# More of the mixer's weight splitting on GpSimd, and another order for the products behind it

## The chip, the cores and the metric

The kernel runs on one core of a Trainium2 chip. Time is microseconds of device time for one execution, the median of three runs. The core's engines are TensorE (PE, with PEld for its weight loads), VectorE (DVE), ScalarE (ACT), GpSimd (POOL) and SyncE (SP), which issues the transfers. Each works through its own queue in order and waits on semaphores of the others.

## What is computed

Two layers over a sequence of 256 rows of 1024 numbers, all in float32. A layer is a SwiGLU feed-forward block (FFN, 2816 wide) at half weight, a token mixer, and a second FFN; after each the sum with the scaled input goes through a layer norm. The mixer projects the row once and feeds three groups of heads:

```python
z = x @ w_in
y_sc  = sc_b * depthwise_conv(sc_c * sc_h, sc_conv_w)        # 3 taps, 256 channels
y_att = banded_window_attention(q, k, v, attn_sink)          # 8 query heads, 2 key heads of 64
u = depthwise_conv(cc_a * sigmoid(cc_gate), cc_conv_w) + cc_conv_b   # 31 taps, 256 channels
y_cc = silu(layer_norm(u, cc_ln_g, cc_ln_b))
out = concatenate([y_sc, y_att, y_cc]) @ w_out
```

## The kernel before

The 256 rows are two tiles of 128 (t = 0, 1). All weights come from HBM as 156 blocks of 128 x 2048 float32 (1 MB), in the order in which they are used. A product of float32 precision is made of three products in a shorter format: each operand is split into a high part (a cast, on ACT, L96) and a low part (operand minus high part, L97), and `mm3` (L153 to L155) adds high x high, low x high and high x low. `emit_block` splits the next block into two of five pairs of buffers; a pair is free for block i when the products with block i-5 have read it. `release` asks for the next split when a block's last product has been issued. In the mixer and at the ends of the FFNs the split goes in four quarters of 128 x 512.

A layer has 33 blocks for the first FFN, 12 for the mixer and 33 for the second FFN. Of the mixer's, 0 and 1 hold the convolution's gate and input, 2 and 3 the queries, 4 keys and values, 5 to 7 the short convolution's three inputs, 8 to 11 the rows of `w_out` (`W_OUT` says which group of heads uses which). In layer 0 they have the numbers 33 to 44 in the order below, so that mixer block 4 is block 37, and blocks 45 to 48 are the first four of the second FFN. Which low parts GpSimd makes instead of DVE is set by `ON_POOL`, counted from the mixer's start:

```python
ON_POOL = range(7, 16)
POOL_BLOCKS = [l * (2 * PER_FFN + PER_MIX) + PER_FFN + i for l in range(DEPTH) for i in ON_POOL]
```

In the mixer TensorE projects and transposes while ACT and DVE do the softmax of four units u (two tiles by two key heads): `S_` scores, `N_` the normalised exponentials, `T_` their transposes, `V_` the product with the values. The 31-tap convolution is 62 DVE instructions (L531, L533), which `fill` puts in portions between the rest. When it is done, `cc_norm` transposes its result and norms it (the reciprocal root on GpSimd, L611), and `cc_out` transposes back, applies swish and splits: that is y[3], the convolution's part of the last product. `w_out(t, h, i)` is six products of head group i for tile t and half h of the 1024 columns; `w_out2(t, i)` does both halves.

Behind the mixer and each FFN but the last stands `boundary`: `part` gives the last products of tile 0, `gather` adds them to the scaled input and takes statistics, `stats` makes the variance on DVE and its reciprocal root on GpSimd (`rstd`, L228), and `apply` scales in two steps on DVE: L233 without the root, L234 with it. Meanwhile TensorE does the products of tile 1. Then `turn(0, h)` transposes the finished tile 0 (L205, reading `x`), and ACT and DVE split it for the next stage. Tile 1 follows in the same way while the next stage's projections (`proj_n`, L181, L182, L185) run on tile 0: `turn(1, 0)` comes behind three of its blocks, `turn(1, 1)` behind the fourth. The order in each queue is what the framework's scheduler makes of the order in which the code is written.

Of the kernel before, what the change touches and what calls it, by code (L numbers as in the profile page):

```python
# [38 lines left out]
PER_MIX = 12  # L39
NBLOCKS = DEPTH * (2 * PER_FFN + PER_MIX)  # L40
W_OUT = (1, 2, 0, 3)
ON_POOL = range(7, 16)
POOL_BLOCKS = [l * (2 * PER_FFN + PER_MIX) + PER_FFN + i for l in range(DEPTH) for i in ON_POOL]


@with_exitstack
def encoder(ctx: ExitStack, tc: tile.TileContext, head_in, xt_in, x_in, w_in, gb_in, small_in, rope_in, out):
# [25 lines left out]
    def big():  # L73
        return hpool.tile([P, 512], F32, tag="big", bufs=6, name="big")

    def bank():
        return acc.tile([P, 512], F32, tag="acc", name="bank")
# [10 lines left out]
    def tmp_bank():  # L88
        return phase["pool"].tile([P, 512], F32, tag="mm", name="tmp")
# [5 lines left out]
    def split(hi, lo, src, eng=None):  # L95
        nc.scalar.copy(hi, src)  # L96
        (eng or nc.vector).tensor_tensor(lo, src, hi.bitcast(F32), ALU.subtract)  # L97
# [42 lines left out]
    def release(delay=2):  # L140
        tasks.append((state["tick"] + delay, emit_block))
# [5 lines left out]
    def tick(parts=1):  # L147
        state["tick"] += 1
        while tasks and tasks[0][0] <= state["tick"]:
            tasks.pop(0)[1](parts)  # L150

    def mm3(ps, ah, al, bh, bl, first, last):
        nc.tensor.matmul(ps, ah, bh, start=first, stop=False)  # L153
        nc.tensor.matmul(ps, ah, bl, start=False, stop=False)  # L154
        nc.tensor.matmul(ps, al, bh, start=False, stop=last)  # L155
# [47 lines left out]
    def transpose(ps, srcs):  # L203
        for i, a in enumerate(srcs):
            nc.tensor.transpose(ps[:, i * P:(i + 1) * P], a, ident)  # L205
# [252 lines left out]
    def mixer(l, norm):  # L458
# [64 lines left out]
        def emit_conv():  # L523
            cacc = chan(big())
            pacc = [tmp_bank() for _ in range(2)]

            def tap(k, c):
                part = pacc[c][:, 0:S]
                dst = cacc[:, c, :] if k == WCC - 1 else part
                if k == 0:  # L530
                    nc.vector.tensor_scalar(dst, upad[:, c, 0:S], wc2[:, c, 0:1], b_cc[:, c:c + 1], op0=ALU.mult, op1=ALU.add)  # L531
                else:
                    nc.vector.scalar_tensor_tensor(dst, upad[:, c, k:k + S], wc2[:, c, k:k + 1], part, op0=ALU.mult, op1=ALU.add)  # L533

            for k in range(WCC):
                for c in range(2):
                    conv.append(lambda k=k, c=c: tap(k, c))
            return cacc
# [51 lines left out]
        def attend(t, i, pT):  # L590
            tk = slice(t * P, (t + 1) * P)
            po = tmp_bank()
            for j in range(2):
                hp = slice(j * HD, (j + 1) * HD)
                for kt in range(NT):
                    nc.tensor.matmul(po[hp, 0:2 * P], vn[kt][:, hp], pT[j][:, kt * 2 * P:(kt + 1) * 2 * P], start=kt == 0, stop=kt == NT - 1)  # L596
            split(y[i][0][:, :, tk], y[i][1][:, :, tk], chan(po[:, 0:2 * P]))

        def cc_norm():
            pus = [tmp_bank() for _ in range(NT)]  # L600
            stat, uns = [], []
            for t, pu in enumerate(pus):
                transpose(pu, [cacc[:, c, t * P:(t + 1) * P] for c in range(2)])
                sts = st.tile([P, 6], F32, tag="sts1", name="sts1")
                mv = st.tile([P, 2], F32, tag="mv", name="mv")
                ve = st.tile([P, 1], F32, tag="ve", name="ve")
                rstd = st.tile([P, 1], F32, tag="rstd", name="rstd")
                nc.vector.bn_stats(sts, pu[:, 0:2 * P])
                nc.vector.bn_aggr(mv, sts)
                nc.vector.tensor_scalar_add(ve, mv[:, 1:2], EPS)  # L610
                nc.gpsimd.tensor_tensor(rstd, ve, mhalf, ALU.pow)  # L611
                stat.append((mv, rstd))
            for pu, (mv, rstd) in zip(pus, stat):
                un = big()
                nc.vector.tensor_scalar(un[:, 0:2 * P], pu[:, 0:2 * P], mv[:, 0:1], rstd, op0=ALU.subtract, op1=ALU.mult)
                uns.append(un)
            return uns

        def cc_out(uns):
            vv, tv = big(), big()  # L620
            for t, un in enumerate(uns):
                pv = tmp_bank()
                transpose(pv, [un[:, 0:P], un[:, P:2 * P]])
                for c in range(2):
                    nc.vector.tensor_scalar(chan(vv)[:, c, t * P:(t + 1) * P], pv[:, c * P:(c + 1) * P], gb2[:, c:c + 1], gb2[:, 2 + c:3 + c],
                                            op0=ALU.mult, op1=ALU.add)
            nc.scalar.activation(tv, vv, AF.Tanh)
            nc.vector.scalar_tensor_tensor(tv, tv, 1.0, vv, op0=ALU.add, op1=ALU.mult)
            split(y[3][0], y[3][1], chan(tv))
# [49 lines left out]
        def T_(u):  # L679
            pTs[u] = p_turned(prs.pop(u)[0])  # L680

        def V_(u):
            attend(u // 2, u % 2, pTs.pop(u))
# [48 lines left out]
        def w_out(t, h, i, ks=(0, 1)):  # L732
            tk = slice(t * P, (t + 1) * P)
            cs = slice(h * 512, (h + 1) * 512)
            for c in ks:
                mm3(accs[t][h], y[i][0][:, c, tk], y[i][1][:, c, tk], wo[W_OUT[i]][0][:, c, cs], wo[W_OUT[i]][1][:, c, cs],
                    (t, h) not in begun, i == 3 and c == 1)
                begun.add((t, h))

        def w_out2(t, i):  # L740
            for h in range(2):
                w_out(t, h, i)
            if t == 1:
                release(1)
            tick()
# [1 line left out]
        w_out2(0, 0)  # L747
        fill(62)
        T_(3)
        w_out2(0, 2)  # L750
        uns = cc_norm()
        V_(3)
        accs.append([bank() for _ in range(2)])
        new_norm = Norm()
        w_out2(1, 2)
        cc_out(uns)
        w_out2(1, 0)
        w_out2(0, 1)

        def part(t, h, piece, cs=(0, 1)):  # L760
            if t == 0:
                if piece == 1:
                    w_out(0, h, 3)
            else:
                w_out(1, h, (1, 3)[piece], cs)
                if h == 1 and 1 in cs:
                    release()

        boundary(accs, new_norm, part)
        return new_norm  # L770

# [3 lines left out]
    for l in range(DEPTH):  # L775
        norm = ffn(l == 0, norm, False)
        norm = mixer(l, norm)
        norm = ffn(False, norm, l == DEPTH - 1)
# [85 lines left out]
```

## Time and profile before

| | |
|---|---|
| median of 3 runs | 935.26 us (935.13 to 937.06) |
| the profiled execution | 937.28 us, span 935.5 us |
| busy: PE, DVE, ACT, POOL | 99%, 69%, 49%, 12% of the span |
| granted clock of TensorE | 0.995 on the mean |
| the two mixers | about 188 to 290 and 650 to 751 us |

The profiled execution's own time is 1.78 us more than its span, which counts from the first to the last instruction of the core. Times below are microseconds from the span's start. A PE that is shown busy is not at its peak: a row of a product is drawn 0.39 us long where the next starts 0.23 us after it.

### The profile page before, as it was taken

To read this page: it belongs to the slowest core of one execution; us is meant where nothing else is said; L and a number is where in the kernel's file an instruction comes from. 1 tells how busy PE (TensorE), PEld (TensorE's weight loads), DVE (VectorE), ACT (ScalarE), POOL (GpSimd) and SP (SyncE) were. 2 spreads that over 40 slices of the span, in tenths; PEclk is the share of its full clock that TensorE was granted. 3 is DMA by queue.
4 is the path that set the end of the run, shared out by engine and by line. 5 is a ranking of instruction groups with operands and counts; after the bars stand their busy time and mean duration, and the time that the engine had idled before them with its cause. 6 is when DMAs were issued, how large, how long until landed. Compare 5 with 4: busy or idle time off the path is not lost.

```text
span 935.5 us, 12113 instructions
## 1 busy us (share of the span) xinstructions
PE 921.8 (99%) x4900; PEld 778.7 (83%) x4900; DVE 645.4 (69%) x811; ACT 458.1 (49%) x593; POOL 116.9 (12%) x108
## 2 busy tenths in 40 slices
PE   9999999999999999999999999999999999999996
PEld 6888888888777888888888888888887788888885
DVE  6966556789967756665777665667799766666545
ACT  6644554345744554445345445454456455444530
POOL 0010000009282000000000000000274800000000
PEclk9999999999999999999999999999999999999998
DMA  9976465546234655454456545544551366555301
GB/s 345 376 249 257 175 222 183 180 140 224 88 102 181 257 211 195 178 187 177 179 187 230 213 180 198 202 171 150 216 190 57 139 247 224 189 180 188 128 1 45
DMA packets 25976, 174.01 MB, mean 186 GB/s; under 512 B 2880, under 2 KB 3136, under 8 KB 5696
## 3 DMA queue, kind: packets, MB, share of 16 engines
q1 hardware_dynamic: 25920, 173.24, 51.5%
q8 instruction: 38, 0.62, 0.3%
q14 instruction: 18, 0.15, 0.0%
HBM read 172.18 MB, written 1.05 MB: 185 GB/s over the span
## 4 chain that ended last, share of the span: by engine, by line
PE 88%; DVE 7%; ACT 1%; POOL 1%; issue 1%; DMA 1%; SPq 0%; DVEq 0%; ACTq 0%
PE wide L170 28%; PE wide L174 15%; PE bank L153 9%; PE bank L154 9%; PE bank L155 9%; PE bank L181 4%; PE bank L185 4%; PE bank L182 4%; DVE tmp L533 3%; PE bank L195 1%; PE tmp L205 1%; POOL lo L97 1%; PE tmp L596 1%; PE bank L205 1%; DVE x L234 1%
## 5 line engine op out<-in xcount | busy, mean ns | idle before, releaser
L97 DVE TENSOR_TENSOR lo<-raw,hi 128x2048 fp32r<-128x2048 f32 (+2 forms) x175 | 317.1, 1825 | 211.1 <-ACT hi L96 210.8
L96 ACT CAST hi<-raw 128x2048 fp32r<-128x2048 f32 (+2 forms) x247 | 306.4, 1270 | 241.2 <-PE wide L170 154.2
L170 PE MATMUL wide<-xT,hi 128*128 128x512 f32 x1152 | 274.1, 390 | 0.0
L170 PEld LDWEIGHTS wide<-xT,hi 128*128 128x128 f32 x1152 | 213.9, 188 | 43.0
L174 PEld LDWEIGHTS wide<-xT,lo 128*128 128x128 f32 x1152 | 147.7, 191 | 5.6
L174 PE MATMUL wide<-xT,lo 128*128 128x256 f32 x1152 | 149.4, 283 | 0.0
L153 PE MATMUL bank<-hi,hh 128*128 128x512 f32 x352 | 137.7, 391 | 0.0
L154 PE MATMUL bank<-lo,hh 128*128 128x512 f32 x352 | 137.4, 390 | 0.0
L155 PE MATMUL bank<-hi,hl 128*128 128x512 f32 x352 | 137.0, 389 | 0.0
L97 POOL TENSOR_TENSOR lo<-raw,hi 128x512 fp32r<-128x512 f32 x72 | 95.9, 1366 | 67.2 <-ACT hi L96 66.8
L228 POOL TENSOR_TENSOR rstd<-ve,mhalf 128x1 f32<-128x1 f32 x12 | 11.5, 961 | 672.0 <-DVE ve L227 672.0
L155 PEld LDWEIGHTS bank<-hi,hl 128*128 128x128 f32 x352 | 66.1, 188 | 14.0
L153 PEld LDWEIGHTS bank<-hi,hh 128*128 128x128 f32 x352 | 66.2, 188 | 12.7
L154 PEld LDWEIGHTS bank<-lo,hh 128*128 128x128 f32 x352 | 66.2, 188 | 12.3
L96 ACT CAST hh<-big 128x512 fp32r<-128x512 f32 x36 | 22.3, 620 | 110.2 <-DVE big L358 110.2
L181 PE MATMUL bank<-hi,xT 128*128 128x512 f32 x160 | 64.7, 404 | 0.0
L182 PE MATMUL bank<-lo,xT 128*128 128x512 f32 x160 | 62.6, 391 | 0.0
L366 DVE TENSOR_TENSOR big<-wide,big 128x512 f32<-128x512 f32 x72 | 49.2, 684 | 6.9 <-ACT big L365 6.9
L533 DVE SCALAR_TENSOR_TENSOR tmp<-upad,wc,tmp 128x256 f32<-128x256 f32 x116 | 49.7, 477 | 0.2
L365 ACT COPY big<-wide 128x512 f32<-128x512 f32 x72 | 42.3, 587 | 11.9 <-PE wide L174 11.6
L185 PE MATMUL bank<-hi,xT 128*128 128x512 f32 x160 | 43.2, 392 | 0.0
L97 DVE TENSOR_TENSOR hl<-big,hh 128x512 fp32r<-128x512 f32 x36 | 24.9, 693 | 24.0 <-ACT hh L96 24.0
(130 smaller groups left out, 890.5 us busy)
## 6 DMA issues: line engine op xcount, KB each, us to landing
raw<-in_w SPq DMA_DIRECT2D x152, 1024.0 KB, 4.8
gb<-in_gb SPq DMA_DIRECT2D x6, 1024.0 KB, 4.9
raw<-in_w SPq DMA_DIRECT2D x4, 512.0 KB, 7.5
head<-in_head SPq DMA_DIRECT2D x4, 384.0 KB, 4.6
raw<-in_w SPq DMA_DIRECT2D x4, 256.0 KB, 7.7
x<-in_x SPq DMA_DIRECT2D x2, 512.0 KB, 5.7
out<-x SPq DMA_DIRECT2D x4, 256.0 KB, 2.1
xraw<-in_xt SPq DMA_DIRECT2D x2, 256.0 KB, 8.0
```

The source lines that it names most:

```text
L96: nc.scalar.copy(hi, src)
L97: (eng or nc.vector).tensor_tensor(lo, src, hi.bitcast(F32), ALU.subtract)
L153: nc.tensor.matmul(ps, ah, bh, start=first, stop=False)
L154: nc.tensor.matmul(ps, ah, bl, start=False, stop=False)
L155: nc.tensor.matmul(ps, al, bh, start=False, stop=last)
L170: nc.tensor.matmul(ps[:, c], w[0][:, k, cs], xT[:, :, k], start=k == 0, stop=False)
L174: nc.tensor.matmul(ps[:, c, 0], w[1][:, k, cs], xT_h[:, k], start=False, stop=k == KC - 1)
L181: nc.tensor.matmul(ps, xT_h[:, kk, t, :], w[0][:, k, :], start=kk == 0, stop=False)
L182: nc.tensor.matmul(ps, xT_h[:, kk, t, :], w[1][:, k, :], start=False, stop=False)
L185: nc.tensor.matmul(ps, xT_l[:, kk, t, :], w[0][:, k, :], start=False, stop=kk == KC - 1)
L366: nc.vector.tensor_tensor(av, ps[:, :, 0], av, ALU.add)
L533: nc.vector.scalar_tensor_tensor(dst, upad[:, c, k:k + S], wc2[:, c, k:k + 1], part, op0=ALU.mult, op1=ALU.add)
```

## The change

`ON_POOL` begins at 4: GpSimd also makes the low parts of the mixer's blocks 4 to 6 (the fifth to the seventh), 12 instructions of 128 x 512 a layer. Between the attention and the boundary the calls change places: `cc_norm` and `V_(3)` come ahead of `w_out2(0, 2)`, `cc_out` comes right behind that, and the two products that stood around it follow. The products of tile 1 with the first attention group, `w_out(1, h, 0)`, leave this place and go into `part` of the boundary, ahead of the others of tile 1. No computation is added or taken away.

```diff
@@ -39,7 +39,7 @@
 PER_MIX = 12
 NBLOCKS = DEPTH * (2 * PER_FFN + PER_MIX)
 W_OUT = (1, 2, 0, 3)
-ON_POOL = range(7, 16)
+ON_POOL = range(4, 16)
 POOL_BLOCKS = [l * (2 * PER_FFN + PER_MIX) + PER_FFN + i for l in range(DEPTH) for i in ON_POOL]
 
 
@@ -747,21 +747,24 @@
         w_out2(0, 0)
         fill(62)
         T_(3)
-        w_out2(0, 2)
         uns = cc_norm()
         V_(3)
+        w_out2(0, 2)
+        cc_out(uns)
         accs.append([bank() for _ in range(2)])
         new_norm = Norm()
+        w_out2(0, 1)
         w_out2(1, 2)
-        cc_out(uns)
-        w_out2(1, 0)
-        w_out2(0, 1)
 
         def part(t, h, piece, cs=(0, 1)):
             if t == 0:
                 if piece == 1:
                     w_out(0, h, 3)
             else:
+                if piece == 0:
+                    w_out(1, h, 0)
+                    if h == 1:
+                        release()
                 w_out(1, h, (1, 3)[piece], cs)
                 if h == 1 and 1 in cs:
                     release()
```


GpSimd's queue at the end of layer 0's first FFN, before; `rstd_782` is the root for tile 0 and `rstd_783` that for tile 1, and the number behind `lo` is the block's:

```order
L228 TENSOR_TENSOR rstd_782<-ve_1512,mhalf_92 128x1
L228 TENSOR_TENSOR rstd_783<-ve_1555,mhalf_92 128x1
L97 TENSOR_TENSOR lo40_1785<-raw40_1580,hi40_1784 128x512 x4
L97 TENSOR_TENSOR lo41_1836<-raw41_1592,hi41_1835 128x512 x4
```


The same place with the change:

```order
L228 TENSOR_TENSOR rstd_782<-ve_1512,mhalf_92 128x1
L97 TENSOR_TENSOR lo37_1595<-raw37_1378,hi37_1594 128x512 x4
L228 TENSOR_TENSOR rstd_783<-ve_1555,mhalf_92 128x1
L97 TENSOR_TENSOR lo38_1730<-raw38_1420,hi38_1729 128x512 x4
L97 TENSOR_TENSOR lo39_1765<-raw39_1466,hi39_1764 128x512 x4
```


The four quarters of block 37 now stand between the two roots. GpSimd's queue at the end of layer 0's mixer, before; `rstd_2426` belongs to tile 0, `rstd_2427` to tile 1:

```order
L97 TENSOR_TENSOR lo46_2441<-raw46_1845,hi46_2440 128x512 x3
L464 TENSOR_SCALAR gb2_5428<-small_94 128x4
L97 TENSOR_TENSOR lo46_2441<-raw46_1845,hi46_2440 128x512
L97 TENSOR_TENSOR lo47_2481<-raw47_1927,hi47_2480 128x512 x4
L228 TENSOR_TENSOR rstd_2426<-ve_2520,mhalf_92 128x1
L97 TENSOR_TENSOR lo48_2579<-raw48_2041,hi48_2578 128x512 x4
L228 TENSOR_TENSOR rstd_2427<-ve_2563,mhalf_92 128x1
```


The same place with the change, where the two roots are `rstd_2454` and `rstd_2455`:

```order
L464 TENSOR_SCALAR gb2_5440<-small_94 128x4
L97 TENSOR_TENSOR lo46_2481<-raw46_1857,hi46_2480 128x512 x4
L228 TENSOR_TENSOR rstd_2454<-ve_2508,mhalf_92 128x1
L97 TENSOR_TENSOR lo47_2579<-raw47_1939,hi47_2578 128x512 x4
L97 TENSOR_TENSOR lo48_2591<-raw48_2053,hi48_2590 128x512 x4
L228 TENSOR_TENSOR rstd_2455<-ve_2563,mhalf_92 128x1
```


Block 47 has gone behind the first root, so that two blocks instead of one stand ahead of the second. TensorE's queue there with the change, from the last product that reads block 42 to the first turn of tile 0 (`x0`):

```order
L155 MATMUL bank_2447<-hi42_1929,yhl_1618 128x512
L153 MATMUL bank_2447<-hi43_2043,yhh_1619 128x512
L154 MATMUL bank_2447<-lo43_2044,yhh_1619 128x512
L155 MATMUL bank_2447<-hi43_2043,yhl_1620 128x512
L153 MATMUL bank_2447<-hi43_2043,yhh_1619 128x512
L154 MATMUL bank_2447<-lo43_2044,yhh_1619 128x512
L155 MATMUL bank_2447<-hi43_2043,yhl_1620 128x512
L153 MATMUL bank_2447<-hi44_2185,yhh_1623 128x512
L154 MATMUL bank_2447<-lo44_2186,yhh_1623 128x512
L155 MATMUL bank_2447<-hi44_2185,yhl_1624 128x512
L205 MATMUL tmp_2551<-ident_85,x0_649 128x128 x4
```


Before, block 42's last product of this kind stood at the end of `w_out2(1, 0)`, ahead of all of tile 0's last products; now nine products are left between it and the turn.

## Rows read from the trace of the kernel before

**Rows 1.** The page, part 1: busy time of each engine, share of the span, instructions
```profile
PE 921.8 (99%) x4900; PEld 778.7 (83%) x4900; DVE 645.4 (69%) x811; ACT 458.1 (49%) x593; POOL 116.9 (12%) x108
```

**Rows 2.** Waits of TensorE in layer 0's mixer, 186:300: total us, times, longest us
```profile
PE tmp L205 <- DVE x L234: 1.1, 2, 0.7
PE bank L548 <- ACT pr L564: 0.6, 2, 0.4
```

**Rows 3.** The same view for layer 1's mixer, 648:760
```profile
PE tmp L205 <- DVE x L234: 0.6, 2, 0.4
```

**Rows 4.** Timeline of TensorE, end of layer 0's mixer: start, us, line, tiles [idle <- by]
```profile
278.70 0.39 PE L154 MATMUL bank<-lo,yhh 128*128 128x512 f32 x1
278.93 0.39 PE L155 MATMUL bank<-hi,yhl 128*128 128x512 f32 x1
...
280.05 0.66 PE L205 MATMUL tmp<-ident,x 128*128 128x128 f32 x4 [0.74 <-DVE x L234]
...
281.01 0.40 PE L155 MATMUL bank<-hi,yhl 128*128 128x512 f32 x1
...
281.74 0.66 PE L205 MATMUL tmp<-ident,x 128*128 128x128 f32 x4 [0.33 <-DVE x L234]
...
290.74 0.60 PE L205 MATMUL tmp<-ident,x 128*128 128x128 f32 x4
```

**Rows 5.** Timeline of TensorE, attention of layer 0, then of layer 1
```profile
235.44 1.75 PE L205 MATMUL bank<-ident,pr 128*128 128x128 f32 x8
...
237.59 0.70 PE L548 MATMUL bank<-kT,qT 64*128 64x256 f32 x2 [0.40 <-ACT pr L564]
...
244.60 1.09 PE L596 MATMUL tmp<-big,vn 128*64 128x256 f32 x8
...
697.88 1.75 PE L205 MATMUL bank<-ident,pr 128*128 128x128 f32 x8
...
705.55 0.66 PE L596 MATMUL tmp<-big,vn 128*64 128x256 f32 x4
```

**Rows 6.** Windows, both layers' second halves: busy by engine, granted clock, DMA share, GB/s
```profile
240.00:262.00 22.00, 22.00 (x144) 17.30 (x144) 19.28 (x49) 15.07 (x44) 11.07 (x12) 0.93 0.15 49
...
702.00:724.00 22.00, 22.00 (x151) 16.59 (x150) 20.25 (x53) 15.39 (x45) 10.15 (x8) 1.00 0.17 53
```

**Rows 7.** Timeline of DVE and of ACT where the convolution begins (layer 0)
```profile
209.85 2.29 DVE L97 TENSOR_TENSOR lo<-raw,hi 128x2048 fp32r<-128x2048 f32 x1 [0.62 <-ACT hi L96]
...
211.35 0.37 ACT L497 COPY upad<-tmp 128x256 f32<-128x256 f32 x1
```

**Rows 8.** Timeline of GpSimd: low parts and reciprocal roots, layer 0, one of layer 1
```profile
192.99 0.99 POOL L228 TENSOR_TENSOR rstd<-ve,mhalf 128x1 f32<-128x1 f32 x1 [6.57 <-DVE ve L227]
...
211.53 21.11 POOL L97 TENSOR_TENSOR lo<-raw,hi 128x512 fp32r<-128x512 f32 x16 [17.55 <-ACT hi L96]
...
256.24 5.16 POOL L97 TENSOR_TENSOR lo<-raw,hi 128x512 fp32r<-128x512 f32 x4 [3.15 <-ACT hi L96]
...
279.41 5.94 POOL L97 TENSOR_TENSOR lo<-raw,hi 128x512 fp32r<-128x512 f32 x4 [0.20 <-ACT hi L96]
...
286.20 1.00 POOL L228 TENSOR_TENSOR rstd<-ve,mhalf 128x1 f32<-128x1 f32 x1 [0.85 <-DVE ve L227]
...
740.40 5.49 POOL L97 TENSOR_TENSOR lo<-raw,hi 128x512 fp32r<-128x512 f32 x4 [0.79 <-ACT hi L96]
```

**Rows 9.** Timeline of DVE: the norms' first and second steps (layer 0)
```profile
192.83 1.40 DVE L233 SCALAR_TENSOR_TENSOR x<-x,mv,gb 128x512 f32<-128x512 f32 x2
...
276.36 2.45 DVE L233 SCALAR_TENSOR_TENSOR x<-x,mv,gb 128x512 f32<-128x512 f32 x2
...
279.25 2.44 DVE L234 SCALAR_TENSOR_TENSOR x<-x,rstd,gb 128x512 f32<-128x512 f32 x2 [0.44 <-POOL rstd L228]
```

**Rows 10.** Timeline of ACT: high part of block 37 (layer 0)
```profile
190.62 2.19 ACT L96 CAST hi<-raw 128x512 fp32r<-128x512 f32 x4
```

**Rows 11.** Timeline of TensorE: second tile's first turn after the first FFN (layer 0)
```profile
198.08 0.60 PE L205 MATMUL tmp<-ident,x 128*128 128x128 f32 x4
```


## The prediction

> **What bounds the kernel now.** The page comes first: TensorE is busy for 921.8 of 935.5 us, no other engine for more than 69% [rows 1]. A change can give back only what TensorE loses, so the waits come next. In layer 0's mixer they hold 1.1 us before the turn of tile 0 behind the mixer, for DVE's second norm step, and 0.6 us in the attention [rows 2]; in layer 1 the turn waits 0.6 us [rows 3]. The timeline shows that this is too little. Products follow each other every 0.23 us (278.70, 278.93), so the first turn could have started at 279.16 and started at 280.05, 0.89 late; the second could have come at 281.24 and came at 281.74, 0.50 late [rows 4]. That is 0.15 to 0.17 more than the idle time of either. Layer 0 so loses 1.4 us there and layer 1 0.9 (0.6 and twice 0.16).
>
> In the attention the eight transposes and what follows them wait for the softmax [rows 5]. From there to the first product with the values layer 0 takes 9.16 us (235.44 to 244.60), layer 1 7.67 (697.88 to 705.55) [rows 5]. The 1.5 us between them are a stretch at the lower clock, 1.2 instead of 2.4 GHz: granted 0.93 over 240 to 262, against 1.00 in layer 1's counterpart [rows 6], and 7% of 22 us is 1.5. It came after the waits of the transposes and scores. The profiled execution, 937.28 us, is 2.0 above the median of 935.26, much as one such stretch would make it. I sum against 937.28 and put the median beside it.
>
> **GpSimd takes three more blocks.** DVE gives up 4 quarters of block 37 and two whole low parts of 2.29 us [rows 7]. This pays nothing by itself. The whole ones end at 212.14, and the convolution that fills DVE from then on cannot start before its padded input is written, 211.35 + 0.37 = 211.72 [rows 7]: 0.3 to 0.4 us is all that moves up, and TensorE waits for none of the three blocks.
>
> On GpSimd a block of four quarters takes 5.16 us undisturbed, and a reciprocal root 0.99 [rows 8]. Where DVE works on two operands from SBUF at the same time both suffer: the block at 279.41 took 5.94 beside a pair of L234 that took 2.44; the one at 740.40 took 5.49 [rows 8, 9]. A pair not so disturbed takes 1.40 [rows 9]. So one DVE instruction adds some 0.39 to the block.
>
> **First place: behind the first FFN, both layers.** The root of tile 1 started at 192.99 [rows 8]; it now stands behind block 37's quarters. The first high quarter is there at 190.62 + 0.55 = 191.2 [rows 10]. In the block's time fall three such DVE instructions, a quarter of block 36 and the two L233 that began at 192.83 [rows 9]. The block ends at 191.2 + 5.16 + 3 x 0.39 = 197.5, the root at 198.5. From the start of L234 to the turn that it releases pass 0.80 us (279.25 to 280.05) [rows 4, 9]: the turn starts at 199.35. TensorE would be there at 198.08 [rows 11] and waits 1.3 us. Bounds: undisturbed 0.1; each of the three adding its whole 0.7, 2.2. I take 1.3 since these three instructions do fall into the block. Their order on DVE has not changed.
>
> **Second place: behind the mixer, both layers.** Moving six products a half of tile 1 behind tile 0's last ones puts 12 x 0.23 = 2.8 us more between the last sum of tile 0 and its turn. The 0.89 and 0.50 go, in layer 1 the 0.9: a gain of 2.3. What is late next is the root of tile 1. Block 47 uses block 42's buffers, and those are now read until nine products before the turn: 279.16 - 9 x 0.23 = 277.1, and 0.2 for the last one to end. Its first high quarter is there at 277.9. Two blocks stand ahead of the root: 2 x 5.16 + 3 x 0.39 (a quarter of block 49, two L233) = 11.5, so 289.4; the root ends at 290.4, and the turn of tile 1 may start at 291.2. Before, block 47 was split earlier and the root started at 286.20 [rows 8]. TensorE reached this turn at 290.74 [rows 4]; without the waits it is there at 289.35 and stops for 1.9 us. Bounds: undisturbed, 290.05, so 0.7; each adding its whole 0.7, 2.8. I take 1.9 for the reason above.
>
> **The rest.** The convolution's norm keeps its place behind the last tap. Between `V_(3)` and tile 0's last products stand 25 products instead of 36, 5.7 us. But ACT and GpSimd no longer split block 46 in between, so y[3] should be there just in time: 0, bounds 0 and 0.5 a layer. In the attention GpSimd now runs from some 205 for six blocks, 6 x 21.11/4 = 31.7 us, to 237, where it stopped at 232.6 [rows 8]. Short two-operand instructions of the softmax at 234 to 237 may each wait for a quarter's end, up to 1.3 us; against it stands the earlier start. I take 0, bounds -0.4 and +1.2 a layer. DMA goes at 0: blocks are fetched five ahead, and the transfers' share is 0.15 to 0.17 there [rows 6].
>
> **Sum.** 2 x 1.3 + 2 x 1.9 - 2.3 = +4.1: 941.4 against the profiled execution, 939.4 against the median. The new stops are longer than those that half clock followed, so I keep one such stretch and forecast 941.0. With all lower ends at the two places, 2 x 0.1 + 2 x 0.7 - 2.3 = -0.7; with the upper ones +7.7.
>
> The Trainium skill (SBUF — State Buffer, section "SBUF: two separate sides") says that a DVE instruction with two SBUF inputs and a GpSimd instruction lock each other out for a whole instruction. By it each of the three would add its full time, an estimate of 0.7 instead of 0.39, and the forecast would be some 4 x 3 x 0.31 = 3.7 higher, 944.7. The rows agree that each waits for the other and show about half the price; the measurement decides.
>
> **Rivals.** (1) The quarters are not held, and the queue costs only its undisturbed time: -0.7, so 936.6, or 934.6 against the median, no change. For it: the port costs in rows 8 are from a few places. Against: the DVE instructions lie in the same 6 us. Chance 0.13. (2) Faster: relief of DVE is what counts. The softmax comes early enough that TensorE's attention waits go, 0.6 idle and at most 1.0 within the transposes' 1.75, and with them the half clock: 936.6 - 3.2 - 1.5 = 931.9. It decides if DVE gains over 1.5 us before the scores; rows 7 leave it 0.4. Chance 0.07. (3) Slower still: GpSimd's longer run meets the softmax, +1.2 a layer, or TensorE drops to half clock after the stops of 1.9, 1.5 us each time: 943.8 to 944.4, with both 946.8. For it: half clock came after shorter waits; against: after the 0.89 and 0.50 it did not. The skill's lock rule ends here too, 944.7. Chance 0.23. The forecast as summed has 0.57.
>
> **Numbers.** 0.2% is 1.9 us, about what a measurement of this kernel can tell from no change. Below 933.4 lies rival 2, within it rival 1: faster 0.07, same 0.13, slower 0.80. The range runs from 936.8 to 945.0: it leaves out rival 2, most of rival 1 and the far end of rival 3.
>
> **What would show it.** Right: TensorE idle before the turns of tile 1, about 1.1 us at 198 and 1.7 near 290, named as DVE's L234, and none before those of tile 0; L228 of tile 1 at some 197.5 and 289.4; low parts at 1.4 us a quarter where L233 lies. Wrong: L228 of tile 1 ahead of 196, or TensorE's waits in the attention gone. Wrong in size: a new wait at `cc_out` or y[3], or the granted clock below 0.99.

## The result, and the profile after the change

The changed kernel takes 942.67 us (median of 4 runs), the kernel before 935.19 (4 runs): a ratio of 1.0071, 95% interval 1.0042 to 1.01. The forecast was 941.0 in a range of 936.8 to 945.0, with 0.80 on slower. One of the four runs, at 957.91 us, was disturbed and stands in no comparison; the other three lie at 942.5 to 942.7. The profiled execution took 942.74 us, span 941.0, against 937.28 and 935.5 before.

The page's first part, columns as in [rows 1]:

```profile
span 941.0 us, 12137 instructions
PE 923.1 (98%) x4900; PEld 780.4 (83%) x4900; DVE 641.5 (68%) x799; ACT 459.8 (49%) x605; POOL 146.1 (16%) x132
```

TensorE is busy 1.3 us longer and its idle time has grown by 4.2; nothing else bounds the kernel. Its waits, layer 0 (186 to 300 us) and then layer 1 (648 to 765), which answer to [rows 2, 3]:

```profile
PE tmp L205 <- DVE x L234: 2.5, 2, 1.7
PE bank L548 <- ACT pr L564: 0.8, 1, 0.8
PE bank L205 <- ACT pr L575: 0.4, 1, 0.4
...
PE tmp L205 <- DVE x L234: 2.6, 2, 1.7
PE bank L548 <- ACT pr L564: 0.8, 1, 0.8
PE bank L205 <- ACT pr L575: 0.4, 1, 0.4
```

Behind L234 TensorE now waits 2.5 us a layer, in two pieces, where it had waited 1.1 and 0.6; in the attention the two rows make 1.2, where 0.6 stood. The turns in TensorE's timeline of layer 0, first of tile 1 behind the FFN, then both of tile 0 and one of tile 1 behind the mixer, which answer to [rows 4]:

```profile
198.43 0.66 PE L205 MATMUL tmp<-ident,x 128*128 128x128 f32 x4 [0.80 <-DVE x L234]
...
280.47 0.60 PE L205 MATMUL tmp<-ident,x 128*128 128x128 f32 x4
...
281.60 0.60 PE L205 MATMUL tmp<-ident,x 128*128 128x128 f32 x4
...
292.12 0.66 PE L205 MATMUL tmp<-ident,x 128*128 128x128 f32 x4 [1.74 <-DVE x L234]
```

Tile 0's turns wait for nothing now; tile 1's two do, 0.80 and 1.74 us. GpSimd's timeline of the same stretches shows why, and how long its run in the convolution has become ([rows 8] before):

```profile
190.68 6.40 POOL L97 TENSOR_TENSOR lo<-raw,hi 128x512 fp32r<-128x512 f32 x4 [4.90 <-ACT hi L96]
197.04 0.55 POOL L228 TENSOR_TENSOR rstd<-ve,mhalf 128x1 f32<-128x1 f32 x1
205.79 30.61 POOL L97 TENSOR_TENSOR lo<-raw,hi 128x512 fp32r<-128x512 f32 x24 [8.20 <-ACT hi L96]
...
279.37 11.40 POOL L97 TENSOR_TENSOR lo<-raw,hi 128x512 fp32r<-128x512 f32 x8 [2.20 <-ACT hi L96]
290.73 0.55 POOL L228 TENSOR_TENSOR rstd<-ve,mhalf 128x1 f32<-128x1 f32 x1
```

Tile 1's roots start at 197.04 and 290.73, each at once behind quarters of low parts; the run of 24 quarters ends at 236.40, where 16 had ended at 232.64. DVE meets the last of them in the softmax. Its timeline there:

```profile
230.19 1.26 DVE L559 SCALAR_TENSOR_TENSOR nm<-mxs,nsink 128x4 f32<-128x4 f32 x1
...
231.76 0.91 DVE L560 TENSOR_TENSOR es<-small,nm 128x4 f32<-128x4 f32 x1
...
234.17 1.02 DVE L570 TENSOR_TENSOR den<-den,es 128x4 f32<-128x4 f32 x1
```

L570 adds four numbers a partition to four others. In the kernel before GpSimd's run was over when it came:

```profile
234.15 0.15 DVE L570 TENSOR_TENSOR den<-den,es 128x4 f32<-128x4 f32 x1
```

Now a quarter is under way, and it takes 1.02 us instead of 0.15. ACT's L575, the transposes and the next scores come that much later. The granted clock behind them, 240 to 262 us and layer 1's counterpart, columns as in [rows 6]:

```profile
240.00:262.00 22.00, 22.00 (x143) 17.19 (x143) 19.59 (x52) 16.35 (x46) 10.02 (x10) 0.92 0.16 58
...
702.00:724.00 22.00, 21.08 (x134) 15.93 (x135) 20.64 (x54) 16.79 (x53) 7.47 (x6) 0.92 0.25 94
```

Both layers have a stretch at 1.2 GHz there; before, one of two had. At 0.92, 8% of 22 us, it costs some 1.7 us.

**Where the time went.** TensorE has 4900 instructions in both kernels, so the starts of the same products can be compared in the two profiled runs, from the first to the last. The changed kernel's run is 0.65 us ahead from about 11 us on, where nothing was changed; the profiled runs of the other versions are ahead by 0 to 1.0 us there, so this is put down to the run and not to the change. The first place costs 1.0 us and 1.05 in the two layers, 2.1 in all; the second 1.9 in each, 3.8. Tile 0's turns and the products just behind them give back 1.8 and 1.4, 3.2. The attention costs 0.9 and 2.4, 3.3: 0.6 of it in each layer is idle time, and most of the rest in layer 1 the additional stretch at half clock. Ahead of the attention 0.2 are gained. With the 0.65 taken off that makes 5.2; the spans differ by 5.5. The medians differ by 7.5, since a typical run of the kernel before has no such stretch and each of the changed kernel two.

### The profile page after: what moved, and what is told of

It reads as the page before. It is cut to its first block, busy times and chain, and to the rows that moved or that the text cites. A ratio compares the mean times of both kernels' runs of the same rounds, so it can differ in the third digit from the quotient of the medians.

```text
span 941.0 us, 12137 instructions
## 1 busy us (share of the span) xinstructions
PE 923.1 (98%) x4900; PEld 780.4 (83%) x4900; DVE 641.5 (68%) x799; ACT 459.8 (49%) x605; POOL 146.1 (16%) x132
## 3 DMA queue, kind: packets, MB, share of 16 engines
HBM read 172.18 MB, written 1.05 MB: 184 GB/s over the span
## 4 chain that ended last, share of the span: by engine, by line
PE 87%; DVE 7%; POOL 3%; ACT 1%; issue 0%; DMA 0%; DVEq 0%; ACTq 0%; POOLq 0%
PE wide L170 28%; PE wide L174 15%; PE bank L153 10%; PE bank L154 10%; PE bank L155 10%; POOL lo L97 3%; DVE tmp L533 3%; PE bank L181 3%; PE bank L182 3%; PE bank L185 3%; PE bank L195 1%; PE tmp L205 1%; PE tmp L596 1%; PE bank L205 1%; DVE big L485 1%; PE bank L398 1%
## 5 line engine op out<-in xcount | busy, mean ns | idle before, releaser
L97 DVE TENSOR_TENSOR lo<-raw,hi 128x2048 fp32r<-128x2048 f32 (+2 forms) x163 | 306.0, 1888 | 205.5 <-ACT hi L96 205.2
L96 ACT CAST hi<-raw 128x512 fp32r<-128x512 f32 (+2 forms) x259 | 308.0, 1221 | 238.7 <-PE wide L170 154.1
L97 POOL TENSOR_TENSOR lo<-raw,hi 128x512 fp32r<-128x512 f32 x96 | 127.3, 1362 | 63.6 <-ACT hi L96 63.4
```

## Experiments

All times are medians, with a 95% interval of the ratio to the kernel before on the same chip, which took 935.7 to 936.9. The 70 runs of it made there fall apart in two: 40 with a mean granted clock of 0.997 or more, median 935.3, and 30 below, median 937.1. The difference, about 1.8, is put down to one stretch at half clock in the attention, which costs some 1.7 in the profiled runs. "Without half clock" below means a mean of 0.997 or more; of runs that were not profiled only the mean is known. Edits are to the changed kernel where nothing else is said.

### order_only: the new order without the three blocks

```diff
-ON_POOL = range(4, 16)
+ON_POOL = range(7, 16)
```

> The new order of the product groups alone; GpSimd keeps blocks 7 to 15 of the mixer, as before the change. My account of the two traces: no wait at the first place (block 37 is not on GpSimd), attention as before the change with no added wait and, as in most runs of it, no stretch at half clock; behind the mixer blocks 47 and 48 still stand ahead of tile 1's root, so TensorE stops there for about 1.7 us (1.9 with what the gaps do not show) in both layers, and the turns of tile 0 no longer wait (2.3 us gained): 935.2 + 3.8 - 2.3 = 936.7. Rival, the order is what costs: most of the change's loss, 941 to 942.7. Rival, the order pays and the queue behind the mixer is the new blocks' doing: 932.9.

938.18 us, 1.0019 (1.0008 to 1.003). The runs lie at 936.5 to 936.8 (four), 938.2 to 938.8 (six) and 939.8. Waits of layer 0 in the profiled run, which was one of the first four; layer 1's are the same to 0.1, without the last row:

```profile
PE tmp L205 <- DVE x L234: 1.7, 1, 1.7
PE bank L548 <- ACT pr L564: 0.6, 2, 0.4
PE tmp L205 <- DVE big L615: 0.2, 1, 0.2
```

The stop at tile 1's turn is there without the three blocks: the account holds in this, and in its number, 936.5 to 936.8 without half clock, forecast 936.7. The new order alone loses 1.2 to 1.5 us. It removes what it was meant to remove, and puts a longer wait at tile 1's turn. The pieces of the sum were other ones: tile 0's turns give back 3.2 and not 2.3, and from the attention to the boundary TensorE takes 0.4 us a layer longer than in the kernel before.

### pool_only: the three blocks in the old order

To the kernel before:

```diff
-ON_POOL = range(7, 16)
+ON_POOL = range(4, 16)
```

> GpSimd's three more blocks alone, with the product order from before the change. My account: tile 1's root behind the first FFN waits for block 37's quarters, 1.0 us of TensorE in each layer; GpSimd's run still goes on when the softmax sums its denominator (L570 about 1.0 instead of 0.15 us), so that TensorE waits some 0.7 to 0.9 us more in the attention and half clock follows, together about 2.0 a layer; behind the mixer as before the change: 935.2 + 2.0 + 4.0 = 941.2. Rival, half clock and attention wait come with the new order: 935.2 + 2.0 = 937.2. Rival, GpSimd's blocks cost nothing once the order is undone: 935.2.

939.29 us, 1.0041 (1.0029 to 1.0053); forecast 941.2. TensorE's waits have the pieces named, 0.85 and 0.84 at the first place, and in the attention idle time of 1.33 and 1.37, but the profiled run has half clock in one layer only: 1.00 in 240 to 262, 0.92 in 702 to 724. By the mean clock all five runs have at least one such stretch. The rivals, 937.2 and 935.2, are out; half clock in both layers was too much, and behind the attention TensorE is 0.6 to 0.7 us a layer faster than in the kernel before (see meet_softmax).

### root_first: quarters behind the root

Blocks 37 and 48 (4 and 15 of the mixer's count, in both layers) are queued on GpSimd behind the latest norm's root; `issue_after` sets the order of issue and no more:

```diff
+AFTER_ROOT = [l * (2 * PER_FFN + PER_MIX) + PER_FFN + i for l in range(DEPTH) for i in (4, 15)]
...
-            split(hi[:, cs], lo[:, cs], raw[:, cs], nc.gpsimd if i in POOL_BLOCKS else None)
+            with tc.issue_after(state["root"].ins) if i in AFTER_ROOT else ExitStack():
+                split(hi[:, cs], lo[:, cs], raw[:, cs], nc.gpsimd if i in POOL_BLOCKS else None)
...
-            nc.gpsimd.tensor_tensor(self.rstd[t], ve, mhalf, ALU.pow)
+            state["root"] = nc.gpsimd.tensor_tensor(self.rstd[t], ve, mhalf, ALU.pow)
```

> The changed kernel, but the low parts of blocks 37 and 48 are queued on GpSimd behind the reciprocal root of tile 1 (issue order only; every instruction of PE and ACT keeps its place). My account: both waits of tile 1's turns go (1.1 and 1.9 us with what the gaps do not show, in both layers), the attention keeps its added waits and its two stretches at half clock: 942.7 - 6.0 = 936.7. Rival, the low parts are then themselves late, TensorE waits for block 48's or block 37's low part instead: 940 to 942.7. Rival, the half clock of the attention follows from the stop at the first place: it goes too, 933.

939.73 us, 1.0035 (1.0023 to 1.0048), with two of five runs at 937.6 and 937.7. Waits of layer 0 (layer 1 the same):

```profile
PE bank L548 <- ACT pr L564: 0.8, 1, 0.8
PE bank L182 <- DVE lo L97: 0.8, 1, 0.8
PE bank L205 <- ACT pr L575: 0.4, 1, 0.4
```

No turn waits any more: both stops came from the queue. But 0.8 us a layer came back in another place. DVE's timeline says how:

```profile
193.26 3.47 DVE L234 SCALAR_TENSOR_TENSOR x<-x,rstd,gb 128x512 f32<-128x512 f32 x2
196.66 3.47 DVE L97 TENSOR_TENSOR lo<-raw,hi 128x512 fp32r<-128x512 f32 x2
```

Block 37's quarters now run beside L234 and beside block 36's quarters on DVE. Each pair takes 3.47 us instead of 1.41 and 1.28 in the changed kernel, and TensorE waits for block 36's last quarter. So a root ahead of block 37 pays only in part; at the second place it costs nothing.

### skip6: one block less in GpSimd's run

```diff
-ON_POOL = range(4, 16)
+ON_POOL = [4, 5, *range(7, 16)]
```

> The changed kernel, but block 39 (number 6 of the mixer) is left to DVE, so that GpSimd's run in the convolution starts at block 40 and ends as before the change, ahead of the softmax's L570. My account: waits of tile 1's turns as in the changed kernel at both places, attention as before the change, L570 at 0.15 us and no half clock in either layer: 942.7 - 4.0 = 938.7. Rival, half clock and attention wait come from the stop at the first place or the new order: 942 to 942.7.

941.15 us, 1.0055 (1.0041 to 1.0069): runs in pairs at 939.2 to 939.5, 941.1 to 941.2 and 942.9 to 943.2. L570 is back at 0.15 us and the attention's waits at 0.40 and 0.22. But half clock did not go: 1.00 in layer 0's stretch, 0.84 in layer 1's, two runs of six without any. The idle time there follows L570; half clock does not follow from L570 alone. A new wait of 0.35 a layer, for L484 at 223.5, makes up the rest.

### order_root: the order, with block 48 behind the root

To root_first:

```diff
-ON_POOL = range(4, 16)
+ON_POOL = range(7, 16)
...
-AFTER_ROOT = [l * (2 * PER_FFN + PER_MIX) + PER_FFN + i for l in range(DEPTH) for i in (4, 15)]
+AFTER_ROOT = [l * (2 * PER_FFN + PER_MIX) + PER_FFN + i for l in range(DEPTH) for i in (15,)]
```

> The new product order alone (GpSimd keeps blocks 7 to 15), with block 48's low parts queued on GpSimd behind the root of tile 1. The new order alone took 936.5 us in its runs without half clock in the attention, 1.7 more for each stretch. My account: its stops at turn(1,0) behind the mixer (1.7 us idle, 1.9 in all, in both layers) go and nothing else moves: 932.7 without half clock, 934.4 with one stretch; faster than before the change by 2. Rival, block 48's low parts are now late and TensorE waits for them behind the turn: 934 to 936.5 without half clock.

934.64 us, 0.9984 (0.9971 to 0.9997). The runs spread from 931.4 to 937.8, three of eleven without half clock (931.4 to 932.9), so that the order does pay 2.4 to 3.9 us against 935.3 once one block stands behind the root. Layer 0's waits hold no turn:

```profile
PE bank L548 <- ACT pr L564: 0.6, 2, 0.4
PE tmp L205 <- DVE big L615: 0.2, 1, 0.2
```

### order_root_eighths: shorter GpSimd instructions

To order_root (block 43 is number 10 of the mixer):

```diff
-            parts = 4
+            parts = 8 if i % (2 * PER_FFN + PER_MIX) == PER_FFN + 10 else 4
```

> As order_root, but block 43, the last of GpSimd's run in the convolution, is cut in eighths instead of quarters (ACT's casts too). Theory, a short DVE instruction with two operands in SBUF waits for the end of the GpSimd instruction that is under way: L559, which took 1.25 us in the kernel before the change against 0.15 undisturbed, takes at most some 0.7; the softmax comes up to 0.5 us sooner a layer: 932.7 - 0.8 = 931.9. Rival, the wait has to do with GpSimd working at all and not with the length of its instruction: L559 stays at 1.25 and the time at 932.7.

930.63 us, 0.9943 (0.9931 to 0.9955), all five runs from 930.0 to 931.1. The timeline of DVE, L559 in order_root first:

```profile
229.78 1.28 DVE L559 SCALAR_TENSOR_TENSOR nm<-mxs,nsink 128x4 f32<-128x4 f32 x1
...
229.25 0.30 DVE L559 SCALAR_TENSOR_TENSOR nm<-mxs,nsink 128x4 f32<-128x4 f32 x1
...
229.86 0.38 DVE L560 TENSOR_TENSOR es<-small,nm 128x4 f32<-128x4 f32 x1
...
231.73 0.58 DVE L570 TENSOR_TENSOR den<-den,es 128x4 f32<-128x4 f32 x1
```

L559 went from 1.28 in order_root to 0.30. GpSimd's run takes 21.68 us instead of 21.14, so it does not work less, only in shorter pieces: here the length of its instruction sets the wait. The attention keeps 0.2 us of idle time in layer 0 and none in layer 1, and half clock is gone with it. That made more than forecast: 4.0 on the medians. This version beats both kernels.

### eighths_again: the same kernel once more

No edit.

> order_root_eighths once more. In order_root_eighths4 and, less, in after_eighths and five_eighths one L559 waited past several ends of GpSimd's eighths (5.4 and 1.8 us) and TensorE for it. If that depends on the order and timing that a kernel's code fixes, this kernel has none of it: 930.0 to 931.2 in nearly all runs, L559 at 0.3 to 0.45. If it comes at random with any eighths, some runs lie at 932 to 936.

930.77 us, 0.9942 (0.9928 to 0.9955), runs from 930.3 to 931.3, L559 0.29 in both layers.

### meet_softmax: the longer run alone

To the kernel before:

```diff
-ON_POOL = range(7, 16)
+ON_POOL = range(6, 16)
```

> The kernel before the change, with one more block on GpSimd (39): its run in the convolution is as long into the softmax as in the changed kernel, but block 37 stays with DVE, so there is no stop at the first place, and the product order is the old one. Theory, half clock follows the longer wait in the attention: TensorE waits some 0.6 us more there in each layer (L570 at 1.0 instead of 0.15), and most runs have one or two stretches at half clock: 934.9 + 1.2 = 936.1 plus 1.7 to 3.4, 937.8 to 939.5. Rival, half clock follows from the stop at the first place: 936.1 in most runs.

935.89 us, 1.0008 (0.9991 to 1.0024), but the runs fall into two groups: six at 934.4 to 935.2, five at 939.1 to 940.6, one between. In the profiled run, which is of the first group, L570 takes 1.00 us and TensorE waits 0.79 for the scores, with no stop at the first place. Half clock comes without that stop (the rival's claim is out), in half of the runs by the mean clock, and for longer in the second group, whose mean is 0.990 to 0.992. The first group is no slower than the kernel before, although TensorE's idle time in the attention is 0.3 us a layer longer, because behind the attention it is 0.6 us a layer faster. Its queue has another order there, although only `ON_POOL` was changed. First the kernel before, then this one:

```profile
260.61 0.38 PE L205 MATMUL tmp<-ident,big 128*128 128x128 f32 x2
260.92 0.65 PE L596 MATMUL tmp<-big,vn 128*64 128x256 f32 x2
261.50 0.44 PE L205 MATMUL tmp<-ident,big 128*128 128x128 f32 x2
261.87 1.08 PE L596 MATMUL tmp<-big,vn 128*64 128x256 f32 x6
...
258.60 0.60 PE L205 MATMUL tmp<-ident,big 128*128 128x128 f32 x4
259.13 1.09 PE L596 MATMUL tmp<-big,vn 128*64 128x256 f32 x8
```

Four transposes and eight products take 2.27 us to the next product before (262.88), and 1.55 here (260.15). Whether the new order of the queue or the work taken off DVE makes the whole of the gain is not shown.

### after_again: the changed kernel once more

No edit.

> The changed kernel once more, for the spread of its runs. Theory, its longer waits in the attention bring half clock in both layers almost every time: 942.6 in nearly all runs. Rival, half clock comes and goes as in the other kernels: runs at 939.2, 940.9 and 942.6.

942.62 us, 1.0077 (1.0065 to 1.0089): 942.4, 942.4, 942.6, 943.5 and 944.5, none without half clock. With the three of the first comparison, eight of eight.

### after_eighths: the changed kernel, blocks 42 and 43 in eighths

```diff
-            parts = 4
+            parts = 8 if i % (2 * PER_FFN + PER_MIX) - PER_FFN in (9, 10) else 4
```

> The changed kernel with blocks 42 and 43, the last two of GpSimd's run in the convolution, cut in eighths instead of quarters; both stops at turn(1,0) stay. Theory, the softmax's short DVE instructions wait for the end of the GpSimd instruction under way, TensorE's waits in the attention follow from that, and half clock follows from those waits: L559 near 0.3, L570 near 0.6, idle before the scores back to some 0.2, and half clock gone: the 930.6 of order_root_eighths plus the stops of 1.1 and 1.9 us in both layers, 936.6. Rival, half clock in the changed kernel follows from its stops at turn(1,0): 940 to 941.5.

939.26 us, 1.0029 (1.0014 to 1.0044). Five of ten runs are without half clock and take 936.9 to 938.7, four of them at most 937.5, near the 936.6 forecast, with both stops in place. That rules the rival out. The others (939.8 to 942.7) have it. In the profiled one L559, L560 and L570 of the first softmax take 0.44, 0.38 and 0.57 us, but one later L559 of layer 1 takes 1.79, past the ends of three eighths; TensorE waits 1.9 for it.

### order_root_eighths4: eighths in four blocks

To order_root:

```diff
-            parts = 4
+            parts = 8 if i % (2 * PER_FFN + PER_MIX) - PER_FFN in (7, 8, 9, 10) else 4
```

> As order_root_eighths, but all four blocks of GpSimd's run in the convolution (40 to 43) in eighths, so that the rotary sums L485, which took 1.82 and 1.38 us against 0.68 and 0.27, wait less too. Theory, those waits delay the convolution and through it the softmax: up to 0.4 us a layer, 929.8 to 930.6. Rival, the extra starts of GpSimd and ACT cost what it saves: 930.6 or some tenths more.

942.99 us, 1.0067 (1.0042 to 1.0092): neither. The rotary sums did fall, 1.82 to 0.99 and 1.40 to 0.28, but GpSimd's run takes 23.55 us instead of 21.14. On DVE and over this whole run:

```profile
229.46 5.42 DVE L559 SCALAR_TENSOR_TENSOR nm<-mxs,nsink 128x4 f32<-128x4 f32 x1
...
211.30 23.55 POOL L97 TENSOR_TENSOR lo<-raw,hi 128x256 fp32r<-128x256 f32 x32 [17.32 <-ACT hi L96]
```

L559 waits past the ends of eight eighths, until GpSimd's run is over (211.30 + 23.55 = 234.85; L559 ends at 234.88), and in layer 1 as long. TensorE stops 2.9 us a layer, and the granted clock is 0.84 over 22 us in both.

### five_eighths: the change without its costs

To order_root:

```diff
-ON_POOL = range(7, 16)
+ON_POOL = range(5, 16)
...
-            parts = 4
+            parts = 8 if i % (2 * PER_FFN + PER_MIX) - PER_FFN in (9, 10) else 4
```

> The change without its three costs: new product order, blocks 5 and 6 of the mixer (38, 39) on GpSimd but not block 4 (37), block 48 behind the root of tile 1, blocks 42 and 43 in eighths. Theory, relief of DVE ahead of the convolution pays nothing by itself and the longer run of GpSimd reaches further into the softmax: 930.6 to 931.5, no faster than order_root_eighths. Rival, with its costs gone the relief pays the 0.5 us by which meet_softmax's undisturbed runs lay below those of the kernel before: 930.

933.85 us, 0.9977 (0.9959 to 0.9994), runs from 930.6 to 938.2, four of twelve without half clock (930.6 to 932.5). The forecast was 930.6 to 931.5. In the profiled run no turn waits, but L559 takes 1.80 in layer 0, until GpSimd's run is over (205.23 + 31.73 = 236.96; L559 ends at 236.99), and TensorE stops 1.94 there:

```profile
235.19 1.80 DVE L559 SCALAR_TENSOR_TENSOR nm<-mxs,nsink 128x4 f32<-128x4 f32 x1
...
205.23 31.73 POOL L97 TENSOR_TENSOR lo<-raw,hi 128x512 fp32r<-128x512 f32 x32 [11.37 <-ACT hi L96]
```

So the cost in the attention was not gone. From there to the boundary TensorE is 0.4 us a layer faster than in order_root_eighths, but no run is below those of that version: two more blocks on GpSimd, with one more in eighths, pay nothing in sum and bring more meetings with the softmax.

## Why the prediction was right, point by point

- **Direction and size.** Forecast 941.0, measured 942.67, inside the range and 1.7 above. Both stops came, at the places and for the cause that were named. That the sum is so near is in part luck: the attention cost 3.3 us where the sum had 0, and against it stand a first place of 2.1 instead of 2.6, 3.2 instead of 2.3 given back at tile 0's turns, and 0.65 us by which the profiled run happened to be ahead from the start.
- **First place.** The block was to end at 197.5 and cost 1.3 a layer; it ended at 197.08 and cost 0.80 of idle time, 1.0 from start to start of the products. The quarters took 6.40, against 5.16 + 3 x 0.39 = 6.33 forecast. What is missing from 1.3 lies in the root, 0.55 us where it follows a low part at once, not 0.99. That no other cause is behind it: the stop is there in pool_only, absent in order_only and root_first.
- **Second place.** 1.9 forecast, 1.74 idle and 1.9 from start to start in both layers. The two blocks took 11.40 against 11.5, and the root started at 290.73, not at 289.4: the stops ahead put this whole stretch about 1 us later than reckoned, TensorE too (ready at 290.23, not at 289.35). The gain of 2.3 at tile 0's turns came in full, and 0.9 more with the products just behind them. order_only shows that this stop belongs to the order, not to the three blocks, as the sum had it.
- **Relief of DVE.** Put at nothing, and y[3] at 0 with a bound of 0.5 a layer. From the attention to the boundary the changed kernel takes as long as the kernel before, to 0.1 us. But the new order alone takes 0.4 us a layer longer there (order_only, order_root), and the blocks on GpSimd alone 0.6 to 0.7 less (pool_only, meet_softmax). So the new blocks did pay something, and the sum had neither: the two cancel in the changed kernel.
- **The attention: the term that was mis-sized.** "Short two-operand instructions of the softmax at 234 to 237 may each wait for a quarter's end" was seen, bounded at +1.2 a layer and taken as 0. It measured 0.6 of idle time a layer. The earlier start that was set against it did not come: TensorE was 0.4 us later than in the run before when the convolution began, by the stop ahead of it, and L559 fell due at 230.19, before at 230.18, and L570 at 234.17, before at 234.15, while GpSimd's run ended at 236.4, near the 237 forecast.
- **Half clock: the other mis-sized term.** "I keep one such stretch" should have been two. Rival 3 put it down to the stops of 1.9; after_eighths has these stops and five runs without half clock. It lies in the attention, right behind the waits there. By the idle time that one profile of each kernel shows there in a layer, these runs had a mean granted clock of 0.997 or more: 9 of 10 at 0.3 or less (order_root_eighths twice; the tenth, at 0.996, is a profiled one and has a granted clock of 1.00 in both layers), 49 of 98 at 0.76 (before, order_only, order_root, skip6), 6 of 12 at 1.0 (meet_softmax), none of 18 at 1.3 to 1.4 (pool_only, root_first, the changed kernel), none of 6 at 3.0 (order_root_eighths4). Two versions have 0.6 in one layer and 2.0 in the other: after_eighths 5 of 10, five_eighths 4 of 12; the stretches of their profiled runs lie in the layer with 2.0. More idle time goes with more half clock. Which of two like runs has it stays open.
- **The lock.** The Trainium skill (SBUF — State Buffer, section "SBUF: two separate sides") has the two engines shut each other out for a whole instruction; by that the forecast was 944.7. On DVE's side the rows agree: L570 lost 0.87 us to a quarter, and the pair of L233 beside block 37 took 3.41 against 1.40 in [rows 9]. On GpSimd's side the block grew by 6.40 - 5.16 = 1.24 for three such instructions, 0.41 each, where whole ones of 0.7 would make 2.1. The estimate of 0.39 was nearer.
- **Rivals.** 1 and 2 are out: the quarters were held, and the attention's waits grew. The first half of rival 3, GpSimd's longer run in the softmax, did come, at half its size.

## What to carry to other kernels

Look in an in-order queue for the small instruction that others wait for: a reciprocal root of 0.55 us behind two blocks of low parts cost 1.9 us, and one block queued behind it gave that back. When a helper engine gets more work, check in the trace which short instructions of its neighbour fall into the longer run; their wait goes by the length of the helper's instruction in most places, and cutting one block in eighths made 4.0 us here, while cutting four lost 8. Compare the order of the queues too: it changed with `ON_POOL` alone, and that stretch with it by 0.6 us a layer. A wait of TensorE can cost more than its idle time: behind waits of 1.3 us in the attention half clock came every time and cost as much again.

## What the runs showed of the hardware that was not expected

- A DVE instruction with two operands in SBUF does not always get in at the end of the GpSimd instruction that is under way. L559 waited for one end in most places (0.3 to 0.45 us with eighths, 1.2 to 1.3 with quarters), but past three in after_eighths and five_eighths (1.8 us) and past eight in order_root_eighths4 (5.42). In all four of these places (order_root_eighths4 has one in each layer) it got in only when GpSimd's whole run was over, 0.02 to 0.03 us behind its end. GpSimd's instructions follow each other without a break there, but also where L559 got in at the first end (order_root_eighths, 229.25). What decides it was not found.
- A GpSimd root that follows a low part at once takes 0.55 us; one that waited for DVE took 0.99.
- Executions of one kernel fall into groups about 1.7 us apart, by their mean clock one stretch at half clock in the attention more or less; fewer waits there narrow the spread as well: 1.1 us over order_root_eighths' five runs, 6.4 over order_root's eleven.
